# A product-key expert layer: tile 1 gathered by rows in place of tile 7, two tiles with scattered gates, and scatter indices loaded on GpSimd's queue

## The chip, the core and the metric

The kernel runs on one core of a Trainium2 chip. Its engines are TensorE (PE in the profile; PEld is its weight load), VectorE (DVE), ScalarE (ACT), GpSimd (POOL) and SyncE (SP, which here only issues DMAs). Each engine works through its own instructions in the order in which they were written to it, and waits for others by semaphores. The metric is the device time of one execution in microseconds.

## The reference

A one-layer encoder on 256 + 1024 tokens of width 1024: retention and latent attention (MLA) side by side, attention to 256 memory tokens, and a layer of single-neuron experts chosen by product keys (PEER). The expert layer is what the change touches. Per token:

```python
q = (xt @ wq).reshape(PEER_BLOCK, PEER_HEADS, PEER_QUERY_DIM)
s1 = jnp.einsum('thd,hkd->thk', q[..., :half], sub_keys[0])   # 8 heads x 128 keys
s2 = jnp.einsum('thd,hkd->thk', q[..., half:], sub_keys[1])
v1, i1 = lax.top_k(s1, 16); v2, i2 = lax.top_k(s2, 16)
cand = v1[..., :, None] + v2[..., None, :]
ts, sel = lax.top_k(cand.reshape(..., 256), 16)               # 16 experts a head, 128 a token
ids = take_along_axis(i1 * 128 + i2, sel); g = softmax(ts)
a = jnp.einsum('td,ted->te', xt, U[ids])
return jnp.einsum('te,ted->td', g * gelu(a), V[ids])          # U, V: 16384 x 1024
```

## The kernel before

The tokens are 10 tiles of 128: tiles 0 and 1 are the short group, 2 to 9 the long one. The program runs in stages:

- projection and retention of all tiles (`phase_a`), MLA of the short group, then "block 0" = tiles 0 and 1 (`phase_b`: output projection, memory attention, the expert layer's queries and scores);
- MLA of the long group (`phase_m`, g = 1), four pairs of heads, some 804 to 1248 us;
- block 1 = tiles 2 to 5 and block 2 = tiles 6 to 9 (`phase_b`);
- the gate stage (`gates`), some 1971 to 2212 us;
- the dense stage (`dense`), to the end.

After the scores of a tile are known, its **routing** (`lists`, `pairs`, `route`: top-16 twice, then the experts' numbers and gates) runs on VectorE. Then a tile takes one of three ways.

- **Gathered by rows** (GATHER, tiles 0, 7, 8, 9): for each of the token's 128 experts GpSimd issues one indirect DMA that brings a row of U to each of 128 partitions (tile `grow`, 4 buffers), and VectorE multiplies and sums it (`gj`); then the same with V (`gps`). That is 256 gathers a tile.
- **Over all experts** (DENSE, the other six): the dense stage computes U x for all 16384 experts on TensorE (`pa`), multiplies by a matrix of gates that is zero but for the chosen experts, and multiplies by V (`pv`, summed into `dacc`).
- The matrix of gates of a dense tile is made in one of two ways. With **scattered gates** (SCATTER, tiles 1, 2, 3) 128 indirect DMAs of GpSimd add each token's gates to a zeroed tensor GS in DRAM (`scatter`, line 1019); their indices and gates are first loaded to `sids` and `sg`, of which there is one buffer each. **On TensorE** (MADE, tiles 4, 5, 6) the gate stage makes, per token, two one-hot matrices (`o1`, `o2`) and one 128x128 matmul, and stores the result to G. Per group of four tokens `o1` is made on VectorE ("v") or ScalarE ("a") by the string O1_BY; `o2` is always VectorE's.

Routing, scatters and gathers are generators. `tick` is called from the main work with an estimate of TensorE's time and takes some steps of them at a share of it, routing first, scatters beside it; `gates` runs the routing of a tile to its end before it uses it, and `dense` runs what is left of the scatters before its first instruction. The order on each engine is then set by a scheduler of the tile framework that places instructions by its own simulated times; it is fixed when the program is built.

The gates of the last MADE tile are not sent through DRAM but kept in SBUF (`self.kept`); the first half of that tile's `pairs` is taken early. SyncE's queue issues nearly all loads and stores, in order: weights (`wraw`, `wl`), scores (`s`, `rs`), `ids`, `ii`, `sids`, `sg`, G, and in the dense stage U and V (`ur`, `vr`). In the dense stage `ur` and `vr` share four buffers, each of which GpSimd frees with its `ul` or `vl`.

Of the kernel before, what the change touches and what calls it, by code (L numbers as in the profile page):

```python
# [28 lines left out]
BLOCKS = [[0, 1], [2, 3, 4, 5], [6, 7, 8, 9]]  # L29
# [4 lines left out]
PH, PK, TK = 8, 128, 16  # L34
# [1 line left out]
EPS, GEPS = 1e-6, 1e-5  # L36
NDEC = RH * P + 5 * RH

GATHER = [0, 7, 8, 9]
DENSE = [t for t in range(NTILE) if t not in GATHER]  # L40
TD = len(DENSE) * P

SCATTER = [1, 2, 3]
MADE = [t for t in DENSE if t not in SCATTER]
TG = 64
HP = PK // 2
NG = 3
O1_BY = ("vaa", "va", "va")

RHO = ((0.75, 0.42), (0.5, 0.0), (0.9, 0.0))  # L50

# [56 lines left out]
class K:  # L108
# [550 lines left out]
    def phase_b(self, sd, blocks, before=None):  # L659

        nc, tc, I = self.nc, self.tc, self.I
        v = self.v
        width = max(len(ts) for ts in blocks) * P
        with ExitStack() as es:
# [74 lines left out]
            for ts in blocks:  # L739
# [95 lines left out]
                order = sorted(ts, key=lambda t: t in GATHER)  # L835
                with tc.tile_pool(name="brt", bufs=1, reuse_waits="tile") as kp:
                    for b in range(4):
                        keys = kp.tile([P, 4, P], F32, tag="keys", name=self.nm("keys"), bufs=2)
                        nc.scalar.dma_start(keys, I["keysT"][:, b * 4:b * 4 + 4, :])
                        ws = self.weights(room, I["peer_wq"], b * 512, 512, keep=kept("peer_wq", b))  # L840
                        qs = [kp.tile([P, 512], F32, tag="pq", name=self.nm("pq"), bufs=5) for j in range(4)]
                        for hf, tt, g, cols in halves:
                            if b == 0:
                                self.transposed(pp, xr[2 * hf:2 * hf + 2], part(a, cols), self.normw[:, 3, :])
                                for j, t in enumerate(tt):
                                    if t in GATHER:
                                        nc.sync.dma_start(sd["x3"][t], xr[2 * hf + j])
                                    else:
                                        sl = slice(hf * 256 + j * P, hf * 256 + (j + 1) * P)
                                        for i in range(2):  # L850
                                            nc.sync.dma_start(sd["x3T"][t][i], r32(a[i][:, :, sl]))

                            def ev(j, ps):
                                nc.scalar.copy(qs[j][:, cols], ps)  # L854
                            wstat(ws, a, cols, ev)
                        for j, t in enumerate(ts):
                            ps = ps_.tile([P, 4, P], F32, tag="s", name=self.nm("s"))
                            for h in range(4):
                                nc.tensor.matmul(ps[:, h, :], qs[h][:, j * P:(j + 1) * P], keys[:, h, :], start=True, stop=True)
                            s = kp.tile([P, 4, P], F32, tag="ks", name=self.nm("ks"), bufs=4)  # L860
                            nc.scalar.copy(s, ps)
                            nc.sync.dma_start(sd["s"][t][:, b * 4:b * 4 + 4, :], s)
                        if b < 3:
                            self.routing.append(self.lists(sd, order[0], b))
                            if b == 1 and order[0] == MADE[-1]:
                                self.routing.append(self.half(0))
                    self.routing.append(self.route(sd, order[0], 3))
                    for t in order[1:]:
# [93 lines left out]
    def route(self, sd, t, b0):  # L962


        nc = self.nc
        v = self.vf
        ap = self.rp
        for b in range(b0, 4):
            yield from self.lists(sd, t, b)
        yield from self.pairs(slice(PH // 2 if t == MADE[-1] else 0, PH))  # L970
        ts, ii = self.rt[3], self.rt[6]
        g = ap.tile([P, PH, TK], F32, tag="g", name=self.nm("g"))
        v.tensor_tensor(g, ts, ts[:, :, 0:1].broadcast_to([P, PH, TK]), ALU.subtract)
# [2 lines left out]
        v.tensor_reduce(sm, g, AX.X, ALU.add)  # L976
        v.reciprocal(sm, sm)
        v.tensor_tensor(g, g, sm.unsqueeze(2).broadcast_to([P, PH, TK]), ALU.mult)
        if t == MADE[-1]:

            self.kept = [ii[:, 0], ii[:, 1], g]
        else:
            nc.sync.dma_start(sd["g"][t], g.rearrange("p h k -> p (h k)"))
# [6 lines left out]
        else:  # L990
            if t in SCATTER:
# [6 lines left out]
                v.tensor_tensor(ids, ii[:, 0].rearrange("p h k -> p (h k)"), ii[:, 1].rearrange("p h k -> p (h k)"), ALU.add)  # L998
                nc.sync.dma_start(sd["ids"][t], ids)
                self.scattering.append(self.scatter(self.gp, sd, t))  # L1000
            elif t != MADE[-1]:
                nc.sync.dma_start(sd["ii"][t], ii.rearrange("p s h k -> p s (h k)"))
        self.routed.add(t)
        yield 0.8
# [2 lines left out]
    def scatter(self, gp, sd, t):  # L1007

        nc, tc = self.nc, self.tc
        ids = gp.tile([P, P], I32, tag="sids", name=self.nm("sids"), bufs=1)  # L1010
        nc.sync.dma_start(ids, sd["ids"][t])
        g = gp.tile([P, P], F32, tag="sg", name=self.nm("sg"), bufs=1)
        nc.sync.dma_start(g, sd["g"][t])
        before = self.zeroed[t]
        for h in range(PH):
            mine = []
# [88 lines left out]
    def gates(self, sd):  # L1105
# [3 lines left out]
        with ExitStack() as es:  # L1109
# [9 lines left out]
            for n, t in enumerate(MADE):  # L1119
                while t not in self.routed:  # L1120
                    self.step()
                if t == MADE[-1]:
                    r = [x.rearrange("p h k -> p (h k)") for x in self.kept]
                else:
                    rt = ap.tile([P, 3, P], F32, tag="r", name=self.nm("r"), bufs=2)
                    nc.sync.dma_start(rt[:, 0:2, :], sd["ii"][t])
                    nc.sync.dma_start(rt[:, 2, :], sd["g"][t])
                    r = [rt[:, j, :] for j in range(3)]
# [8 lines left out]
                for q in range(P // TG):  # L1137
                    st = ap.tile([P, HP, 2, TG], F32, tag="st", name=self.nm("st"), bufs=2)
                    self.late = self.anchor
                    for k in range(0, TG, 4):  # L1140
# [2 lines left out]
                        pt = pg.tile([P, 4, P], F32, tag="pt", name=self.nm("pt"))  # L1143
                        o1s = ap.tile([P, 4, P], F32, tag="o1", name=self.nm("o1"), bufs=6)
                        c0 = q * TG + k
                        by = O1_BY[n]
                        who = by[(c0 // 4) % len(by)]
                        if who == "v":
                            v.tensor_tensor(o1s, rT[:, 0, c0:c0 + 4].unsqueeze(2).broadcast_to([P, 4, P]),
# [245 lines left out]
```

## Time and profile before

| | |
|---|---|
| three runs | 4538.4, 4547.82, 4554.45 us, median 4547.82 us |
| profiled execution | 4537.65 us, of which span 4535.9 us |
| busy, share of the span | PE 87%, PEld 77%, DVE 68%, POOL 59%, ACT 33% |
| L1019, scatters | 384 instructions, 620.7 us of GpSimd |
| L1063, row gathers | 512 of U and 512 of V, 529.5 and 510.1 us of GpSimd |
| dense stage, matmuls `pa` and `pv` | 2048 and 1536 of each of three kinds, the same before and after the change |

A row of a view names the line, the engine, the operation and the tiles (out<-in, without buffer numbers). Busy times are of one engine; idle time stands with what ended it. An instruction is charged to the line that issued it; VectorE's go through two helpers, so that line 74 holds the main work and line 90 the routing and the gathers.

### The profile page before, as it was taken

Reading aid. Unit: us, or ns where it says so; the run is one execution under the profiler, and the core shown is the slowest. Engines: PE = TensorE matmul, PEld = TensorE weight load, DVE = VectorE, ACT = ScalarE, POOL = GpSimd, SP = SyncE. Lnnn points to the kernel's source line nnn. Section 1 sums busy time; section 2 is a strip of 40 time slices with the busy share of each in tenths; the row PEclk is TensorE's granted clock in tenths of the full one; section 3 lists DMA queues with packets and bytes.
Section 4 is the critical chain, followed back from the end, with each engine's and each line's share of the span. In section 5 each row is a group of like instructions: output and inputs, shape, how many; then the busy total and the mean of one; then the engine's idle time right before and its main releaser. Section 6 shows DMA issues by size and latency. Waiting matters only on the chain.

```text
span 4535.9 us, 64896 instructions
## 1 busy us (share of the span) xinstructions
PE 3937.6 (87%) x22425; PEld 3477.2 (77%) x22425; DVE 3073.4 (68%) x6808; ACT 1517.1 (33%) x3256; POOL 2677.9 (59%) x2283
## 2 busy tenths in 40 slices
PE   7999988856788989285599999999999999999998
PEld 7999867644577888274577888888888888888887
DVE  5565432844566498176399877777877777777778
ACT  5333544433434343065222222222222222222222
POOL 2230243178666557777436766776767777677775
PEclk9999998988899999698799999999999999999999
DMA  4422577124678867476637888989989989899887
GB/s 147 168 72 87 201 264 276 29 12 87 204 251 264 279 166 193 80 172 124 172 111 239 304 292 304 314 306 308 312 312 310 310 310 309 304 315 310 304 306 262
DMA packets 534843, 1030.49 MB, mean 227 GB/s; under 512 B 100848, under 2 KB 235504, under 8 KB 534512
## 3 DMA queue, kind: packets, MB, share of 16 engines
q0 software_dynamic: 204832, 545.55, 38.4%
q1 hardware_dynamic: 306928, 445.11, 30.0%
q10 hardware_dynamic: 22752, 35.68, 2.2%
q8 instruction: 176, 2.88, 0.3%
q14 instruction: 155, 1.27, 0.1%
HBM read 901.68 MB, written 124.45 MB: 226 GB/s over the span
## 4 chain that ended last, share of the span: by engine, by line
DMA 20%; POOL 14%; issue 11%; DVE 10%; PE 2%; ACT 1%; SPq 0%; POOLq 0%; DVEq 0%; ACTq 0%
DMA grow<-in_peer_v,gids 7%; DMA grow<-in_peer_u,gids 6%; POOL grow L1063 5%; POOL GS L1019 4%; DMA ur<-in_uT 3%; POOL vl L1245 3%; DVE gps L90 3%; POOL ul L1221 2%; DVE dacc L74 1%; DVE gj L90 1%; DVE oh L90 1%; DMA vr<-in_peer_v 1%; DVE wr L74 1%; DVE wl L74 1%; DMA GS<-sg,sids 1%
## 5 line engine op out<-in xcount | busy, mean ns | idle before, releaser
L1019 POOL DMA_INDIRECT GS<-sg,sids x384 | 620.7, 1616 | 314.6 <-DMA sids<-ids 142.7
L90 DVE SCALAR_TENSOR_TENSOR gps<-grow,ga,gps 128x1024 f32<-128x1024 f32 x512 | 657.4, 1284 | 218.4 <-DMA grow<-in_peer_v,gids 210.1
L1063 POOL DMA_INDIRECT grow<-in_peer_u,gids x512 | 529.5, 1034 | 354.1 <-DVE gj L90 222.2
L170 PE MATMUL pa<-dxT,uh 128*128 128x384 f32 x2048 | 690.0, 337 | 15.4 <-ACT uh L1220 12.8
L1063 POOL DMA_INDIRECT grow<-in_peer_v,gids x512 | 510.1, 996 | 321.8 <-DVE gps L90 206.1
L172 PE MATMUL pa<-dxT,ul 128*128 128x384 f32 x2048 | 682.1, 337 | 7.7 <-POOL ul L1221 7.4
L171 PE MATMUL pa<-dxT,uh 128*128 128x384 f32 x2048 | 688.0, 336 | 0.0
L170 PE MATMUL pv<-vh,wh 128*128 128x512 f32 x1536 | 612.0, 401 | 80.1 <-DVE dacc L74 73.4
L171 PE MATMUL pv<-vl,wh 128*128 128x512 f32 x1536 | 615.3, 401 | 20.6 <-POOL vl L1245 20.3
L172 PE MATMUL pv<-vh,wl 128*128 128x512 f32 x1536 | 607.6, 396 | 0.0
L90 DVE SCALAR_TENSOR_TENSOR gj<-grow,gps 128x1024 bf16<-128x1024 f32 x384 | 467.3, 1217 | 185.4 <-DMA grow<-in_peer_u,gids 170.7
L203 POOL TENSOR_TENSOR wl<-wraw,wh 128x512 fp32r<-128x512 f32 x180 | 239.5, 1349 | 342.8 <-ACT wh L199 241.4
L1221 POOL TENSOR_TENSOR ul<-ur,uh 128x512 fp32r<-128x512 f32 x256 | 338.3, 1329 | 148.6 <-ACT uh L1220 141.7
L170 PEld LDWEIGHTS pv<-vh,wh 128*128 128x128 f32 x1536 | 293.0, 191 | 165.2 <-DVE dacc L74 99.9
L170 PEld LDWEIGHTS pa<-dxT,uh 128*128 128x128 f32 x2048 | 386.2, 189 | 29.6 <-ACT uh L1220 17.0
L170 PE MATMUL pj<-act,wh 128*128 128x256 f32 x1088 | 311.6, 295 | 107.0 <-ACT pq L854 88.3
L172 PEld LDWEIGHTS pa<-dxT,ul 128*128 128x128 f32 x2048 | 385.1, 188 | 22.2 <-POOL ul L1221 19.0
L171 PEld LDWEIGHTS pa<-dxT,uh 128*128 128x128 f32 x2048 | 386.3, 189 | 4.2
L171 PEld LDWEIGHTS pv<-vl,wh 128*128 128x128 f32 x1536 | 293.1, 191 | 103.0 <-POOL vl L1245 49.7
L1245 POOL TENSOR_TENSOR vl<-vr,vh 128x512 fp32r<-128x512 f32 x256 | 328.3, 1301 | 68.6 <-ACT vh L1244 55.7
L90 DVE SCALAR_TENSOR_TENSOR gj<-grow,gx 128x1024 bf16<-128x1024 f32 x128 | 191.3, 1494 | 234.3 <-DMA grow<-in_peer_u,gids 233.0
L1220 ACT CAST uh<-ur 128x512 fp32r<-128x512 f32 x256 | 158.7, 621 | 550.0 <-DMA ur<-in_uT 517.9
(287 smaller groups left out, 8761.6 us busy)
## 6 DMA issues: line engine op xcount, KB each, us to landing
ur<-in_uT SPq DMA_DIRECT2D x256, 256.0 KB
vr<-in_peer_v SPq DMA_DIRECT2D x256, 256.0 KB
GS<-zero ACTq DMA_DIRECT2D x24, 1024.0 KB
wraw<-in_peer_wq SPq DMA_DIRECT2D x96, 256.0 KB
G<-st SPq DMA_DIRECT2D x48, 512.0 KB
gt<-GS SPq DMA_DIRECT2D x192, 128.0 KB
gt<-G SPq DMA_DIRECT2D x64, 384.0 KB
wraw<-in_w_out SPq DMA_DIRECT2D x48, 256.0 KB
```

The lines of the kernel that those rows point to most:

```text
L74: r = f(*a, **kw)
L90: r = f(*a, **kw)
L170: mm(ps, a[0], b[0], start=first, stop=False)
L171: mm(ps, a[0], b[1], start=False, stop=False)
L172: mm(ps, a[1], b[0], start=False, stop=last)
L203: (nc.vector if self.spare and k in self.spare else eng).tensor_tensor(wl[:, :n], raw[:, :n], r32(wh[:, :n]), ALU.subtract)
L1019: r = nc.gpsimd.indirect_dma_start(out=sd["GS"][t].rearrange("l a g h (t o) -> (l a g h t) o", o=1), in_=g[:, s:s + 1], in_offset=None, ou ...
L1063: nc.gpsimd.indirect_dma_start(out=u, out_offset=None, in_=src, in_offset=bass.IndirectOffsetOnAxis(ap=ids[:, s:s + 1], axis=0))
L1220: nc.scalar.copy(uh, ur)
L1221: nc.gpsimd.tensor_tensor(ul, ur, r32(uh), ALU.subtract)
L1245: nc.gpsimd.tensor_tensor(vl, vr, r32(vh), ALU.subtract)
```

## The change

Tile 1 changes places with tile 7: tile 1 is now gathered by rows, tile 7 goes over all experts with its gates made on TensorE. Two tiles (2, 3) have scattered gates in place of three, four (4 to 7) are made on TensorE in place of three. The tile whose `pairs` are halved (HALVED, still 6) and the one whose gates are kept in SBUF (KEPT, now 7) are no longer the same. `o1` is split evenly between VectorE and ScalarE for every tile. The loads of `sids` and `sg` move from SyncE's queue to GpSimd's.

```diff
-GATHER = [0, 7, 8, 9]
+GATHER = [0, 1, 8, 9]
...
-SCATTER = [1, 2, 3]
+SCATTER = [2, 3]
 MADE = [t for t in DENSE if t not in SCATTER]
+HALVED, KEPT = [t for t in MADE if t in BLOCKS[-1]][0], MADE[-1]
...
-O1_BY = ("vaa", "va", "va")
+O1_BY = "va"
...
-                            if b == 1 and order[0] == MADE[-1]:
+                            if b == 1 and order[0] == HALVED:
                                 self.routing.append(self.half(0))
...
-        yield from self.pairs(slice(PH // 2 if t == MADE[-1] else 0, PH))
+        yield from self.pairs(slice(PH // 2 if t == HALVED else 0, PH))
...
-        if t == MADE[-1]:
+        if t == KEPT:
             self.kept = [ii[:, 0], ii[:, 1], g]
...
         ids = gp.tile([P, P], I32, tag="sids", name=self.nm("sids"), bufs=1)
-        nc.sync.dma_start(ids, sd["ids"][t])
+        nc.gpsimd.dma_start(ids, sd["ids"][t])
         g = gp.tile([P, P], F32, tag="sg", name=self.nm("sg"), bufs=1)
-        nc.sync.dma_start(g, sd["g"][t])
+        nc.gpsimd.dma_start(g, sd["g"][t])
```

The order of the instructions moves at three places. The first is GpSimd's queue in the long group's MLA, behind its loads of the latents (`lat`). Before:

```order
L553 DMA lat_9615<-lat_69 128x768
L1019 DMA GS_183<-sg_10354,sids_10352 2097152x1 x64
L1063 DMA grow_11214<-in_peer_u,gids_11204 128x1024
L1063 DMA grow_11248<-in_peer_u,gids_11204 128x1024
L1063 DMA grow_11318<-in_peer_u,gids_11204 128x1024
L1063 DMA grow_11349<-in_peer_u,gids_11204 128x1024
L1019 DMA GS_183<-sg_10354,sids_10352 2097152x1 x13
L1063 DMA grow_11398<-in_peer_u,gids_11204 128x1024
```

Now (all line numbers are two higher):

```order
L555 DMA lat_9605<-lat_69 128x768
L1065 DMA grow_11178<-in_peer_u,gids_11168 128x1024
L1065 DMA grow_11211<-in_peer_u,gids_11168 128x1024
L1065 DMA grow_11280<-in_peer_u,gids_11168 128x1024
L1065 DMA grow_11310<-in_peer_u,gids_11168 128x1024
L1065 DMA grow_11358<-in_peer_u,gids_11168 128x1024
```

Tile 1's 128 scatters are gone from between tile 0's row gathers; 43 gathers stand in this stage before and after.

The second is SyncE's queue in block 2, while the expert layer's query weights are loaded. Before, the load of the third scatter's indices stands between these loads:

```order
L194 DMA wraw_19728<-in_peer_wq 128x512
L194 DMA wraw_19734<-in_peer_wq 128x512
L1011 DMA sids_22451<-ids_123 128x128
L194 DMA wraw_19740<-in_peer_wq 128x512
L1013 DMA sg_22453<-g_133 128x128
L983 DMA g_135<-g_19427 128x128
```

Now it stands on GpSimd's queue, between the last scatter of tile 2 and the first of tile 3:

```order
L1021 DMA GS_183<-sg_16710,sids_16708 2097152x1 x128
L1065 DMA grow_19518<-in_peer_u,gids_11168 128x1024
L1065 DMA grow_19906<-in_peer_u,gids_11168 128x1024
L1065 DMA grow_20098<-in_peer_u,gids_11168 128x1024
L1065 DMA grow_20129<-in_peer_u,gids_11168 128x1024
L1013 DMA sids_23088<-ids_123 128x128
L1015 DMA sg_23090<-g_133 128x128
L1065 DMA grow_20164<-in_peer_u,gids_11168 128x1024
L1065 DMA grow_20198<-in_peer_u,gids_11168 128x1024
L1021 DMA GS_184<-sg_23090,sids_23088 2097152x1 x2
L1065 DMA grow_20232<-in_peer_u,gids_11168 128x1024
L1021 DMA GS_184<-sg_23090,sids_23088 2097152x1 x11
```

In SyncE's queue six more loads of these weights now pass before the queue comes to a store (`ii` of tile 5) that needs VectorE's routing; before, `sids` was reached with 21 of this block's 32 loads issued, now `ii` with 27.

The third is VectorE's queue in the gate stage. The routing of tile 7, which before stood in the dense stage, now ends directly ahead of that tile's first one-hot matrices; the last rows of it now are

```order
L92 TENSOR_TENSOR oh_22436<-oh_22436 128x64x4
L92 TENSOR_TENSOR oh_22436<-oh_22436 128x64x2
L92 TENSOR_TENSOR ii_21896<-oh_22436 128x64
L76 TENSOR_SCALAR nT_22456<-rT_22454 128x128
L76 TENSOR_TENSOR o_4611_22464<-rT_22454,io 128x512
L76 TENSOR_SCALAR o_4612_22466<-io,rT_22454 128x128
```

Here `oh` and `ii` are the routing's last step and `nT` and `o` the gate stage's own. The number of row gathers inside the dense stage is the same, 125 of V of tile 0 and 256 for each of three tiles; the last of ScalarE's conversions that run ahead into the gate stage (`uh`, the third) stands behind 82 of 96 copies `st` before and behind 115 of 128 now.

## Rows read from the trace of the kernel before

**Rows 1.** The page's second part: the span in 40 slices of 113.4 us, busy tenths of TensorE and the clock that TensorE was granted.

```profile
PE   7999988856788989285599999999999999999998
PEclk9999998988899999698799999999999999999999
```

**Rows 2.** Busy time by stretch (stretch, its length, busy time of each engine with its count of instructions, granted clock, DMA share, GB/s): the four pairs of heads of the long group's attention, one stretch each.

```profile
804.00:886.00 82.00, 71.34 (x401) 52.03 (x400) 74.39 (x321) 43.61 (x81) 0.00 (x0) 0.94 0.08 25
886.00:966.00 80.00, 74.29 (x438) 53.59 (x438) 69.16 (x266) 42.98 (x82) 59.62 (x37) 0.96 0.28 26
966.00:1127.00 161.00, 78.06 (x432) 54.84 (x430) 53.38 (x102) 42.18 (x79) 131.52 (x87) 0.76 0.39 63
1127.00:1248.00 121.00, 96.33 (x515) 67.91 (x514) 66.85 (x126) 49.18 (x96) 76.20 (x58) 0.87 0.67 193
```

**Rows 3.** From 886 to 1183 us, while the first scatter runs: what VectorE waited for (total us, times, longest), and GpSimd's two groups of instructions (count, busy us, mean ns, idle time before them).

```profile
DVE gj L90 <- DMA grow<-in_peer_u,gids: 111.2, 16, 50.2
L1019 POOL DMA_INDIRECT GS<-sg,sids x128 | 209.5, 1637 | 152.8 <-DMA sids<-ids 107.1 <-issue 43.1 <-DMA GS<-sg,sids 1.6
L1063 POOL DMA_INDIRECT grow<-in_peer_u,gids x27 | 28.8, 1065 | 8.2 <-issue 7.3 <-DMA GS<-sg,sids 0.6 <-DVE ob L74 0.3
```

**Rows 4.** In order of time (start us, length us, then what; in brackets the idle time before it and what ended it): GpSimd's first row gather, and the VectorE instruction that waited for that gather.

```profile
1017.79 1.00 POOL L1063 DMA_INDIRECT grow<-in_peer_u,gids  x1 [0.30 <-issue]
...
1022.22 1.23 DVE L90 SCALAR_TENSOR_TENSOR gj<-grow,gx 128x1024 bf16<-128x1024 f32 x1 [50.23 <-DMA grow<-in_peer_u,gids]
```

**Rows 5.** Waits from 1500 to 1910 us (who, for whom, total us, times, longest us), the engines' and SyncE's queue.

```profile
DVE gj L90 <- DMA grow<-in_peer_u,gids: 106.0, 4, 93.7
ACT wh L199 <- DMA wraw<-in_peer_wq: 104.8, 12, 87.6
...
SPq L1011 <- DMA GS<-sg,sids: 95.2, 4, 89.8
```

**Rows 6.** In order of time: the first and the last instruction of the second scatter and the first of the third on GpSimd; SyncE's load of the third scatter's indices; and VectorE's first instruction of the gate stage.

```profile
1632.52 1.63 POOL L1019 DMA_INDIRECT GS<-sg,sids  x1 [35.63 <-DMA sids<-ids]
...
1898.88 1.54 POOL L1019 DMA_INDIRECT GS<-sg,sids  x1 [0.30 <-issue]
1913.93 1.89 POOL L1019 DMA_INDIRECT GS<-sg,sids  x1 [0.30 <-issue]
...
1901.95 0.33 SPq L1011 DMA_DIRECT2D sids<-ids  x1
...
1978.87 0.23 DVE L74 TENSOR_SCALAR nT<-rT 128x128 f32<-128x128 f32 x1 [18.14 <-ACT rT L1133]
```

**Rows 7.** Busy time by stretch, columns as in rows 2: the gate stage before, in and after its stop.

```profile
1975.00:2112.00 137.00, 106.62 (x697) 92.79 (x697) 133.06 (x497) 126.86 (x334) 100.60 (x62) 0.93 0.81 185
2112.00:2197.00 85.00, 0.65 (x3) 0.65 (x4) 0.81 (x3) 1.81 (x5) 64.99 (x43) 0.51 0.26 14
2197.00:2215.00 18.00, 17.30 (x112) 16.65 (x112) 14.01 (x62) 12.94 (x33) 0.16 (x1) 0.87 0.96 276
```

**Rows 8.** The gate stage's groups (count, busy us, mean ns, idle time before): one-hot halves and copies on ScalarE, both one-hot halves on VectorE.

```profile
L74 DVE TENSOR_SCALAR o<-io,rT 128x128 f32<-128x128 f32 x384 | 108.6, 363 | 85.1 <-PE pt L1164 84.4
L74 DVE TENSOR_TENSOR o<-rT,io 128x512 f32<-128x512 f32 x43 | 29.2, 679 | 0.0
L1157 ACT ACTIVATE o<-io,nT 128x128 f32<-128x128 f32 x212 | 69.4, 416 | 0.3 <-DVE nT L74 0.3
L1158 ACT ACTIVATE o<-o 128x512 f32<-128x512 f32 x53 | 33.8, 646 | 0.0
L1166 ACT COPY st<-pt 128x512 f32<-128x512 f32 x96 | 55.1, 597 | 4.0 <-DMA G<-st 1.9 <-PE pt L1164 1.4
```

**Rows 9.** Around the gate stage's stop: a wait of SyncE's queue (2090 to 2200 us), and the scatter's instructions with VectorE busy (2000 to 2090 us, first row) and idle (2113 to 2192 us, second row).

```profile
SPq L1217 <- POOL ul L1221: 93.8, 2, 92.2
...
L1019 POOL DMA_INDIRECT GS<-sg,sids x43 | 72.0, 1674 | 20.6 <-issue 12.5 <-DMA GS<-sg,sids 8.2
...
L1019 POOL DMA_INDIRECT GS<-sg,sids x40 | 61.7, 1542 | 17.8 <-issue 15.4 <-DMA GS<-sg,sids 2.5
```

**Rows 10.** In order of time: the last scatter instruction on GpSimd, and VectorE's last instruction of the gate stage and its first of the dense stage.

```profile
2189.35 1.54 POOL L1019 DMA_INDIRECT GS<-sg,sids  x1 [0.30 <-issue]
...
2211.58 0.28 DVE L90 FIND_INDEX8 ti<-tv,rs 128x8 uint32<-128x128 f32 x1
2231.35 2.23 DVE L74 TENSOR_TENSOR wr<-wr,gt 128x384 f32<-128x384 f32 x2 [19.48 <-DMA gt<-GS]
```

**Rows 11.** Busy time of VectorE in the instructions of line 90 alone, over the whole span, and the page's three groups of that line that belong to the gathers.

```profile
0.00:4540.00 4540.00, 1792.21 (x3969) 0.94 0.71 227
...
L90 DVE SCALAR_TENSOR_TENSOR gps<-grow,ga,gps 128x1024 f32<-128x1024 f32 x512 | 657.4, 1284 | 218.4 <-DMA grow<-in_peer_v,gids 210.1
L90 DVE SCALAR_TENSOR_TENSOR gj<-grow,gps 128x1024 bf16<-128x1024 f32 x384 | 467.3, 1217 | 185.4 <-DMA grow<-in_peer_u,gids 170.7
L90 DVE SCALAR_TENSOR_TENSOR gj<-grow,gx 128x1024 bf16<-128x1024 f32 x128 | 191.3, 1494 | 234.3 <-DMA grow<-in_peer_u,gids 233.0
```

**Rows 12.** Busy time by stretch, columns as in rows 2: two stretches of the dense stage.

```profile
2235.00:3000.00 765.00, 716.33 (x3484) 635.40 (x3485) 632.41 (x1314) 195.96 (x355) 471.35 (x417) 0.97 0.78 263
3000.00:4000.00 1000.00, 953.38 (x4685) 839.76 (x4684) 773.70 (x934) 255.81 (x467) 704.73 (x647) 0.99 0.90 308
```

**Rows 13.** One line's instructions on one tensor (count, shortest, median and longest in ns, first and last start in us): plain loads that GpSimd issues.

```profile
L553 POOL DMA_DIRECT2D lat<-lat x8: 537/538/573, 771.0 to 783.8; - x8
```

More of the change, by code (lines that the diff above doesn't have):

```diff
@@ L1000, in route @@
                 self.scattering.append(self.scatter(self.gp, sd, t))
-            elif t != MADE[-1]:
+            elif t != KEPT:
                 nc.sync.dma_start(sd["ii"][t], ii.rearrange("p s h k -> p s (h k)"))
@@ L1121, in gates @@
                     self.step()
-                if t == MADE[-1]:
+                if t == KEPT:
                     r = [x.rearrange("p h k -> p (h k)") for x in self.kept]
@@ L1145, in gates @@
                         c0 = q * TG + k
-                        by = O1_BY[n]
+                        by = O1_BY
                         who = by[(c0 // 4) % len(by)]
```

## The prediction

> **What bounds the kernel now.** I read the page's slices first. TensorE is busy eight or nine tenths almost throughout, with two kinds of holes: two slices near 1000 us at five and six tenths and slices at about 1870 and 2160 us at two and five, and the granted clock falls there too [rows 1]. The dense stage, from slice 21 on, is full. So the question is what the change does to these holes and what it adds.
>
> The first hole is in the long group's attention. Its four pairs of heads are the same work, but take 82, 80, 161 and 121 us [rows 2]. What differs is in the waits of VectorE: it waits 111.2 us, 16 times, for rows of U [rows 3]. These rows are gathered on GpSimd, and in its queue tile 1's scatter stands ahead of and between the gathers: 128 instructions of 1637 ns against 27 gathers of 1065 ns [rows 3]. The first gather starts at 1017.79 us, and VectorE, which reached its use about 50 us earlier, goes on at 1022.22 [rows 4]. VectorE works in order, so the softmax behind that product waits too, and TensorE with it.
>
> The second hole is in block 2. SyncE waits 89.8 us to load the third tile's indices, because `sids` has one buffer and the second scatter is still reading it; behind it in the queue are the query weights, and ScalarE waits 87.6 us for those [rows 5]. But VectorE is held in the same time as well, 93.7 us, by one row gather [rows 5] that stands in GpSimd's queue behind the same 128 scatters. The scatter runs from 1632.52 to 1898.88, the indices are loaded at 1901.95, the gate stage begins at 1978.87 [rows 6].
>
> The third hole, 85 us, is in the gate stage [rows 7]: SyncE waits 92.2 us for GpSimd to free a buffer of `ur` [rows 9], and GpSimd does so only behind the third scatter, at 2189.35 [rows 10]. ScalarE's `uh` for that load stands ahead of the last copies of the gates, so the gates stop.
>
> **Term 1, tile 1's scatter: -100 us.** All 128 scatters go from the attention stage; nothing takes their place there, since tile 1's rows are gathered in the dense stage, where tile 7's were. Two readings price it: VectorE's waits, 111.2 us [rows 3], and the pace, 161 + 121 against 82 + 80, that is 120 us [rows 2]. Pace is the upper end, since it also counts the product instructions themselves. What is late next is the gathers' own latency: 4.4 us from the first one's start to its use [rows 4], hidden by four buffers when 41 gathers are spread over some 170 us. I take 100, a little under the waits, because VectorE will wait for some of the 27. The low end is 50: only the first long wait goes, and the others covered something else on TensorE or ScalarE.
>
> **Term 2, the indices on GpSimd's queue: -10 us at the start of the gate stage, and +2.** This removes SyncE's wait but not VectorE's: the row gather still stands behind the second scatter. In the new order SyncE gets six more of this block's weight loads out and then stops at a store that needs VectorE. So the hole becomes shorter by TensorE's work on six of 32 loads, and what it can give the gate stage is bounded by the 18.14 us that VectorE waited there for TensorE's late end of the block [rows 6]. I take 10 of 0 to 18, as one row gather now stands behind 13 scatters of the third tile, where it stood behind 7. GpSimd's four new loads cost 538 ns each [rows 13], 2 us in all; behind each wait scatters and gathers, and the landing they wait for is the one that they waited for before. The whole hole counted as gain, 84 us, would be a mistake: the end of the next stage hangs on the scatters, which start no earlier relative to block 1.
>
> **Term 3, a fourth tile of gates and tile 7's routing: +20 us.** VectorE was busy 133.06 + 14.01 us in the gate stage [rows 7]. Added are one tile of `o2`, 108.6 / 3 = 36 us; 64 in place of 43 `o1`, 21 x 679 ns = 14 us [rows 8]; and a tile's routing, line 90 less its gathers over ten tiles, (1792.2 - 657.4 - 467.3 - 191.3) / 10 = 48 us [rows 11]. Together 245 us. ScalarE has less: for a tile 16 of its `o1` at (69.4 + 33.8) / 53 = 1.95 us and copies of 55.1 / 3 = 18 us, 50 us, four times 200 [rows 8]; so VectorE sets the stage. Before, the stage took 1978.87 to 2211.58 [rows 6, 10], 233 us, with 85 of them the stop. The new work fills the stop. Counted from the second scatter's last instruction (1898.88), the gates begin at +70, `uh` is reached after 115 of 128 copies at +70 + 220 = +290, and the third scatter ends at +290 before, some +300 now; so a stop of about 10 us is left. The stage takes 245 + 10 = 255, 22 more than before; I count 20. Low end 0 (the model of VectorE is too full), high end 97: none of the new work fits into the stop.
>
> A rule of the Trainium skill speaks against this step. Scatters with VectorE busy take 1674 ns and with it idle 1542 [rows 9]; 128 of them all under the gates make at most 17 us, of which the third scatter bore more than half already, and the +300 holds the rest. The page "SBUF — State Buffer", section "SBUF: two separate sides", says that a DMA issued by GpSimd needs descriptors written by it, and that some two-port VectorE instructions lock it out meanwhile, so that such a DMA belongs on another queue. By that the scatter would stretch further under four tiles of `o2`, and the stop grow; by the rows it costs 0.13 us an instruction.
>
> **Term 4, the dense stage: -3 us.** TensorE's work and the number of gathers are unchanged, and a tile's routing less stands on VectorE. In the first stretch, with three routings, 3484 matmuls take 765 us, at the later pace (4685 in 1000 us) they would take 744 [rows 12]: 21 us, 7 for each routing at most, 0 at least. I take 3.
>
> **The sum.** -100 - 10 + 2 + 20 - 3 = -91 on the profiled execution, 4537.65 us, of which 4535.9 are span: 4447 us. That execution is 10 us below the median of the three runs and just below their fastest; I move up by 3 and say 4450.
>
> **Rivals.**
>
> 1. The gate stage's stop stays whole. It would if the third scatter ended some 75 us later against the gates than I count, or if another `ur` stood in front of earlier copies. For it: the same queues meet there as before. Against: 115 of 128 copies now stand ahead of `uh`. The price is the other 75 us of the 85: 4525. Chance 0.09.
> 2. Only the first wait in the attention stage goes (50 of the 100 us): 4500. For it: TensorE has only 78 us of work in the 161 of the third pair, so something else could be late next. Against: the first two pairs ran in 82 and 80 us with VectorE busy 74 and 69 of them [rows 2]. Chance 0.12.
> 3. The hole in block 2 closes, because VectorE reaches the held gather later than TensorE needs it. Then the gates end before the third scatter, and that bounds: the stage ends at +300 and a few copies in place of +325, 25 us earlier: 4425. Chance 0.09.
> 4. Slower. The attention stage's pace is set by the landing of the gathered rows and not by their place behind the scatters, so that term 1 gives 10 at most, while the fourth tile's gates and the routing (98 us) lie open behind the stop: 4537.65 - 10 + 97 = 4625. It decides where term 1 is smaller than term 3. For it: a wait that is put down to a DMA may be the transfer itself. Against: the gather of 1017.79 had landed 4.4 us later [rows 4]. Chance 0.04.
>
> That the change does not do what it says is excluded for the attention stage by the order; for the hole in block 2 it is what term 2 says.
>
> **How the numbers follow.** The forecast has 0.66: its own spread is -120 to -80 for term 1 and 0 to +30 for term 3, so 4417 to 4480. The range, 4405 to 4500, takes in rivals 2 and 3 and the sum with 50 or 120 for term 1; rivals 1 and 4 lie outside. Runs of this kernel differ by about 0.3%, 14 us, and less than that counts as the same: 4534 to 4561. All cases but rival 4 lie below 4534, and of rival 1 (4525) a third may reach it: faster 0.92, same 0.04, slower 0.04.
>
> **What will show it.** The four pairs of heads should take some 80 us each, with VectorE's waits for rows of U under 20 us there. The second scatter should start some 100 us earlier, at about 1532. VectorE should still wait about 90 us for one row gather in block 2, and TensorE still stop, for 40 to 70 us, with SyncE now at the store of `ii`. The gate stage should have VectorE busy for about 245 us with a stop of at most 20 us. The dense stage should start 75 to 100 us earlier and last as long as before, within 10 us. The prediction is wrong if the third pair still takes over 110 us, if the gate stage still stops for over 50, or if the dense stage changes by more than 20.

## The result and the profile after

| | before | after |
|---|---|---|
| median of the runs (us) | 4551.14 (4538.4 to 4557.76) | 4433.91 (4422.06 to 4437.58) |
| ratio to before, 95% interval | | 0.9741 (0.9712 to 0.977) |
| profiled execution (us), its span | 4537.65, 4535.9 | 4435.69, 4433.9 |
| PE busy | 3937.6 (87%) | 3971.3 (90%) |
| GpSimd busy | 2677.9 (59%) | 2475.2 (56%) |

The change made the kernel faster, by 117 us in the medians and by 102 us between the two profiled executions. The kernel before has a fourth run here, beside the three given above. The line numbers of after are two higher than those of before. The page's slices of after, TensorE and the clock granted to it (they answer to [rows 1]):

```profile
PE   7999888899889986476899999999999999999998
PEclk9999999899899998688999999999999999999999
```

The hole at slices 8 and 9 (counted from 0) is gone, and the clock no longer falls there. Of the other two, the one at 18 and 19, the gate stage's stop, has become a stage with TensorE at seven and six tenths (slices 17 and 18); the one in block 2 stays, in slices 15 and 16, about 1740 to 1860 us. Four places of the trace show where the 102 us went.

**The attention of the long group.** Its four pairs of heads by stretch, each from one pair's first instruction to the next one's (stretch, length, busy time of PE, PEld, DVE, ACT and POOL with counts, granted clock, DMA share, GB/s), as in [rows 2]:

```profile
806.00:889.00 83.00, 70.99 (x405) 51.21 (x404) 75.06 (x328) 43.91 (x81) 0.05 (x1) 0.94 0.09 26
889.00:967.00 78.00, 72.87 (x431) 52.73 (x430) 70.89 (x264) 42.45 (x81) 7.21 (x8) 0.96 0.20 64
967.00:1040.00 73.00, 70.93 (x434) 51.01 (x433) 53.91 (x105) 43.46 (x81) 20.25 (x18) 1.00 0.45 139
1040.00:1138.00 98.00, 87.10 (x517) 62.66 (x515) 60.18 (x116) 48.63 (x95) 32.63 (x29) 0.95 0.67 224
```

Together 332 us, where it was 444. The waits from 889 to 1138 us (who, for whom, total us, times, longest), the stretch that answers to [rows 3], and GpSimd's first gather (start, length; in brackets the idle time before it):

```profile
POOL grow L1065 <- DMA gids<-ids: 102.3, 1, 102.3
POOL grow L1065 <- DVE st L76: 73.7, 9, 52.7
...
DVE ob L76 <- ACT ob L595: 20.5, 8, 3.6
...
888.95 1.01 POOL L1065 DMA_INDIRECT grow<-in_peer_u,gids  x1 [102.32 <-DMA gids<-ids]
```

VectorE's wait for rows of U, 111.2 us before, no longer appears, and its longest total is the 20.5 us shown; now GpSimd waits for VectorE. The gather that started at 1017.79 [rows 4] starts at 888.95.

**Block 2.** Waits from 1390 to 1830 us, of the engines and of SyncE's queue, which answer to [rows 5]:

```profile
DVE gj L92 <- DMA grow<-in_peer_u,gids: 110.3, 10, 96.5
ACT wh L201 <- DMA wraw<-in_peer_wq: 104.6, 13, 84.6
PE pj L172 <- ACT pq L856: 84.0, 4, 82.4
...
SPq L1004 <- DVE ii L92: 93.8, 1, 93.8
```

TensorE still stops for 82.4 us. The instructions around this stop in order of time, from the timelines of GpSimd, VectorE and SyncE's queue, as in [rows 6]: the second scatter's first and last instruction, VectorE's held product, GpSimd's loads of the indices and gates, the third scatter's first, SyncE's held store, and VectorE's first instruction of the gate stage:

```profile
1515.52 1.65 POOL L1021 DMA_INDIRECT GS<-sg,sids  x1 [3.65 <-DMA sids<-ids]
...
1791.20 1.55 POOL L1021 DMA_INDIRECT GS<-sg,sids  x1 [0.30 <-issue]
...
1797.47 1.23 DVE L92 SCALAR_TENSOR_TENSOR gj<-grow,gx 128x1024 bf16<-128x1024 f32 x1 [96.52 <-DMA grow<-in_peer_u,gids]
...
1797.83 0.62 POOL L1013 DMA_DIRECT2D sids<-ids  x1
1798.41 0.63 POOL L1015 DMA_DIRECT2D sg<-g  x1
...
1803.95 1.62 POOL L1021 DMA_INDIRECT GS<-sg,sids  x1 [0.56 <-DMA sg<-g]
...
1812.59 0.32 SPq L1004 DMA_DIRECT2D ii<-ii  x1
...
1862.30 0.23 DVE L76 TENSOR_SCALAR nT<-rT 128x128 f32<-128x128 f32 x1 [7.48 <-ACT rT L1135]
```

SyncE's queue no longer stops at `sids` but, for 93.8 us, at the store of `ii`, which needs VectorE's routing, and VectorE stands at a row gather behind the scatter, as before.

**The gate stage.** The whole stage as one stretch, its groups (count, busy us, mean ns, idle time before; the last is the scatters), and GpSimd's last scatter and VectorE's first product of the dense stage; they answer to [rows 7], [rows 8] and [rows 10]:

```profile
1862.00:2107.00 245.00, 175.90 (x1069) 152.59 (x1068) 238.76 (x950) 181.75 (x460) 173.73 (x106) 0.86 0.74 167
...
L76 DVE TENSOR_SCALAR o<-io,rT 128x128 f32<-128x128 f32 x512 | 149.1, 368 | 0.2
L76 DVE TENSOR_TENSOR o<-rT,io 128x512 f32<-128x512 f32 x64 | 43.3, 678 | 0.0
L1021 POOL DMA_INDIRECT GS<-sg,sids x103 | 170.1, 1652 | 43.3 <-issue 28.3 <-DMA GS<-sg,sids 14.7 <-PE pt L1166 0.3
...
2072.92 1.55 POOL L1021 DMA_INDIRECT GS<-sg,sids  x1 [0.30 <-issue]
...
2123.87 1.03 DVE L76 TENSOR_TENSOR wr<-wr,gt 128x384 f32<-128x384 f32 x2 [18.95 <-DMA gt<-G]
```

The stop of 85 us [rows 7] is gone: VectorE is busy 238.76 of 245 us, and its one-hots wait 0.2 us where they waited 85.1 [rows 8]. From the stage's first instruction to the dense stage's first product it is 261.6 us, where it was 252.5 [rows 6, 10].

**The dense stage.** Two stretches of it, as in [rows 12], and TensorE's last matmul:

```profile
2128.00:2893.00 765.00, 722.84 (x3538) 641.33 (x3539) 616.04 (x1098) 195.71 (x357) 492.31 (x441) 0.98 0.82 278
2893.00:3893.00 1000.00, 944.06 (x4618) 830.38 (x4617) 767.43 (x938) 253.02 (x458) 697.76 (x641) 0.99 0.89 304
...
4425.23 0.39 PE L174 MATMUL pv<-vh,wl 128*128 128x512 f32 x1
```

Against before, the stages begin or end as follows (start of the matmuls behind the attention 1252.97 and 1138.63; before's last matmul ended at 4527.84; the others from the rows above and [rows 6, 10]):

| | before | after | difference |
|---|---|---|---|
| block 1 begins on TensorE | 1252.97 | 1138.63 | -114.3 |
| second scatter's first instruction | 1632.52 | 1515.52 | -117.0 |
| second scatter's last instruction | 1898.88 | 1791.20 | -107.7 |
| gate stage, VectorE's first | 1978.87 | 1862.30 | -116.6 |
| dense stage, VectorE's first | 2231.35 | 2123.87 | -107.5 |
| TensorE's last matmul ends | 4527.84 | 4425.62 | -102.2 |

So the whole gain is made before 1253 us; the gate stage gives 9 us back and the dense stage 5.

### The profile page after: what moved, and what is told of

Read it like the earlier page. It is cut to its first block, busy times and chain, and to the rows that moved or that the text cites. A ratio compares the mean times of both kernels' runs of the same rounds, so it can differ in the third digit from the quotient of the medians.

```text
span 4433.9 us, 65461 instructions
## 1 busy us (share of the span) xinstructions
PE 3971.3 (90%) x22684; PEld 3508.8 (79%) x22684; DVE 3111.2 (70%) x6954; ACT 1558.1 (35%) x3344; POOL 2475.2 (56%) x2159
## 5 line engine op out<-in xcount | busy, mean ns | idle before, releaser
L1021 POOL DMA_INDIRECT GS<-sg,sids x256 | 420.1, 1641 | 123.6 <-issue 97.7
L174 PEld LDWEIGHTS pv<-vh,wl 128*128 128x128 f32 x1536 | 294.2, 192 | 57.3
L1237 ACT CAST wh<-wr 128x384 fp32r<-128x384 f32 x256 | 130.7, 513 | 580.9 <-DVE wr L76 575.4
```

Source lines behind the costliest of these rows:

```text
L174: mm(ps, a[1], b[0], start=False, stop=last)
L1021: r = nc.gpsimd.indirect_dma_start(out=sd["GS"][t].rearrange("l a g h (t o) -> (l a g h t) o", o=1), in_=g[:, s:s + 1], in_offset=None, ou ...
L1237: nc.scalar.copy(wh, wr)
```

## The experiments

Ratios are to the kernel before, run on the same chip beside each group of four.

### Where the gain comes from: the queue of the index loads, or tile 1's scatter

The first kernel undoes one part of the change:

```diff
-        nc.gpsimd.dma_start(ids, sd["ids"][t])
+        nc.sync.dma_start(ids, sd["ids"][t])
...
-        nc.gpsimd.dma_start(g, sd["g"][t])
+        nc.sync.dma_start(g, sd["g"][t])
```

> The changed kernel with the scatter indices and gates loaded on SyncE's queue again, as before the change. Theory: VectorE's row gather behind the second scatter holds block 2 whichever queue the indices are on, so this costs 0 to 10 us: 4434 to 4445 us, ratio to the kernel before 0.974 to 0.977, TensorE's stop in block 2 again about 84 us and starting some 20 us earlier against the end of the second scatter. Rival: SyncE's wait was what held block 2, and moving the loads is worth most of the 84 us: 4500 to 4515 us, ratio 0.989 to 0.992.

It took 4434.45 us, ratio 0.9744 (0.9718 to 0.977): no different from the changed kernel. Its waits from 1390 to 1860 us, and TensorE's first matmul behind the stop in block 2: before, in the changed kernel, and here (in brackets the stop):

```profile
DVE gj L92 <- DMA grow<-in_peer_u,gids: 126.4, 13, 95.3
SPq L1013 <- DMA GS<-sg,sids: 94.8, 4, 89.3
...
1908.80 0.58 PE L170 MATMUL pj<-act,wh 128*128 128x256 f32 x1 [83.90 <-ACT pq L854]
...
1822.37 0.58 PE L172 MATMUL pj<-act,wh 128*128 128x256 f32 x1 [82.43 <-ACT pq L856]
...
1794.29 0.58 PE L174 MATMUL pj<-act,wl 128*128 128x256 f32 x1 [83.86 <-DMA wl<-wl_peer_wq]
```

TensorE's stop is 83.9 us, where it is 82.4 in the changed kernel, and the gates begin at 1861.5. What differs is where the stop lies against the second scatter's last instruction (1898.88 before, 1791.20 in the changed kernel, 1783.80 here). Before and here it runs from 74 and 73 us ahead of that instruction to 10 us behind it; in the changed kernel, from 51 us ahead to 31 us behind. So the six weight loads do make the stop begin 22 us later, as expected, but it also ends 21 us later. With the loads on SyncE the queue goes on as soon as the scatter has ended; in the changed kernel it goes on at 1812.59, when VectorE has done the routing that stands behind the gather of 1797.47. The move of the loads shifts the stop and does not shorten it, and in the time it is worth nothing that these runs show.

The second takes the kernel before and leaves out tile 1's 128 scatters alone:

```diff
-                self.scattering.append(self.scatter(self.gp, sd, t))
+                if t == 1:
+                    self.scattered[t] = self.zeroed[t]
+                else:
+                    self.scattering.append(self.scatter(self.gp, sd, t))
```

> The kernel before with the 128 scatter instructions of tile 1 left out, so that tile 1's gates stay zero; nothing else is changed. Theory: the attention stage becomes 105 to 117 us shorter and all that follows comes earlier by that and lasts as long as before: 4434 to 4446 us, ratio 0.974 to 0.977. Rival: the attention stage's gain is partly eaten later, because the chain of the two other scatters does not move along: 4480 to 4500 us, ratio 0.985 to 0.989.

4432.51 us, 0.9748 (0.9719 to 0.9777). Leaving out the one scatter gives as much as the whole change. But the work behind it is different: here the gate stage has three tiles and still stops. Its waits from 1860 to 2110 us:

```profile
PE pt L1167 <- ACT st L1169: 86.3, 3, 85.7
ACT uh L1223 <- DMA ur<-in_uT: 85.7, 1, 85.7
```

Its dense stage begins at 2117.30, only 6.6 us before that of the changed kernel. So the fourth tile of gates and a tile's routing, 98 us of VectorE by the prediction's count, fill a stop of 85 and cost 7 on top (10 if each stage is counted from its own first instruction).

### What bounds the stages between: the held gather, the third scatter, or VectorE

The third kernel takes no row gathers into GpSimd's order while a scatter is under way (in two places):

```diff
-        while self.owed > 0.0 and (self.routing or self.gathering):
+        while self.owed > 0.0 and (self.routing or self.gathering and not self.scattering):
```

> The changed kernel with no row gathers taken up while a scatter is pending, so that nine gathers of U move behind the third scatter. Theory: VectorE is not held in block 2, TensorE's stop of 82 us there goes and the gate stage starts some 80 us earlier, but the third scatter still ends where it did (10 us earlier at most), the gate stage stops for it again, and the dense stage starts 40 us behind it, as in the kernel before: 15 to 20 us gained, 4410 to 4420 us, ratio 0.969 to 0.971. Rival A: the scatters are no bound, and the 82 us come through: 4350 us, ratio 0.956. Rival B: something else holds block 2: 4434 us, ratio 0.974.

4427.84 us, 0.9741 (0.9711 to 0.9771). The stop in block 2 is gone and the gates begin 87 us earlier, at 1775.3. They then stop for the third scatter, whose last instruction starts at 2070.64: ScalarE's `uh` waits for a load of `ur`, whose buffer GpSimd frees behind the scatter. The gate stage by stretch, before and in this stop, and that wait:

```profile
1775.00:2004.00 229.00, 160.59 (x961) 135.67 (x960) 221.93 (x887) 167.20 (x424) 171.53 (x104) 0.87 0.69 150
2004.00:2079.00 75.00, 0.00 (x0) 0.00 (x0) 2.03 (x7) 2.49 (x7) 57.51 (x38) 0.53 0.25 19
...
ACT uh L1222 <- DMA ur<-in_uT: 75.0, 1, 75.0
```

The dense stage begins at 2114.27, 9.6 us earlier than in the changed kernel. Of 82 us of stop removed in block 2, 75 come back in the gate stage. The bound is the theory's. Of the 15 to 20 us that it gave, the start of the dense stage shows about half and the time none: the ratio is that of the changed kernel, 0.9741.

The fifth kernel (the fourth comes below) is this one with the index loads on SyncE again, the edit of the first experiment.

> The kernel without the held gather (e3) with the scatter indices and gates on SyncE's queue. Theory: two waits cover each other in block 2, VectorE's gather and SyncE's index load; with the first gone the second alone holds the weights, so that TensorE's stop of some 80 us in block 2 is back, and the gate stage starts at about 1855 us and not at 1775. The time grows little, since the third scatter bounds the stage's end: 4428 to 4440 us, ratio 0.973 to 0.976. Rival: with VectorE free there is no stop in block 2 on either queue, and the time is that of e3, 4428 us, with gates from 1775 us.

4426.4 us, 0.9729 (0.968 to 0.9778). TensorE's longest wait from 1390 to 1860 us (of its weight loads), SyncE's from 1500 to 1900 us, and the gate stage as one stretch:

```profile
PEld pj L174 <- DMA wl<-wl_peer_wq: 78.7, 2, 77.6
...
SPq L1013 <- DMA GS<-sg,sids: 86.0, 4, 80.6
...
1858.00:2105.00 247.00, 177.06 (x1063) 151.25 (x1063) 238.91 (x950) 181.21 (x458) 163.27 (x99) 0.87 0.71 162
```

The stop in block 2 is back at 77.6 us, with no gather held. So two waits covered one another there: VectorE's for the gather and SyncE's for `sids`. Each keeps the stop alone, VectorE's in the changed kernel and SyncE's in this run, and only with both gone does it close (the third). The total does not tell the two kernels apart, but not for the reason expected. In this one the gates begin at 1857.8, VectorE is busy 238.91 of 247 us, and the third scatter's last instruction starts at 2062.19: as in the changed kernel VectorE's gates come last, and the dense stage begins at 2123.7. In the third kernel the gates begin 83 us earlier, the third scatter comes last, and the dense stage begins 9.5 us earlier.

The fourth kernel is the changed one with less work in the last tile's gates: of every 64 tokens only the first four get one-hots and matmuls, and the gates of the others are copies of theirs.

```diff
-                        pt = pg.tile([P, 4, P], F32, tag="pt", name=self.nm("pt"))
-                        o1s = ap.tile([P, 4, P], F32, tag="o1", name=self.nm("o1"), bufs=6)
+                        if not (t == KEPT and k):
+                            pt = pg.tile([P, 4, P], F32, tag="pt", name=self.nm("pt"))
+                            o1s = ap.tile([P, 4, P], F32, tag="o1", name=self.nm("o1"), bufs=6)
...
+                        if t == KEPT and k:
+                            nc.scalar.copy(st[:, :, :, k:k + 4], st[:, :, :, 0:4])
+                            continue
```

> The changed kernel with most of tile 7's gates left out: of every 64 tokens only the first four get one-hot matrices and matmuls, and their result is copied for the others; routing, copies and stores stay. Theory: VectorE has 44 us less in the gate stage, but the third scatter then bounds, so that the dense stage starts 40 us behind its end: 10 us gained, 4420 to 4428 us, ratio 0.971 to 0.973. Rival A: VectorE alone sets the stage's end: 44 us gained, 4390 us, ratio 0.965. Rival B: the gates' work was wholly covered: 4434 us.

4418.05 us, 0.9703 (0.9674 to 0.9732). VectorE's first product of the dense stage, the last scatter, and two stretches of SyncE's queue:

```profile
2104.45 2.11 DVE L76 TENSOR_TENSOR wr<-wr,gt 128x384 f32<-128x384 f32 x2 [40.29 <-DMA gt<-GS]
...
2073.73 1.55 POOL L1021 DMA_INDIRECT GS<-sg,sids  x1 [0.30 <-issue]
...
2067.84 27.00 SPq L1120 DMA_DIRECT2D G<-st  x16
...
2098.32 0.95 SPq L1216 DMA_DIRECT2D gt<-GS  x2
```

VectorE now waits 40 us for the scattered gates, and the dense stage begins 19 us earlier than in the changed kernel; the time falls by 16, which the two intervals do not separate. So in the changed kernel VectorE's gates come last. The size lies between what the theory and the rival expected, nearer the theory, but the theory's bound is not what shows. The third scatter's last instruction has ended at 2075.28, and the first loads of the scattered gates are issued at 2098.32, behind 16 stores of G that keep SyncE's queue busy for 27 us. The edit left these stores in and let them come all at once. How far the third scatter's chain lies behind VectorE's gates in the changed kernel is not shown by this run; that it bounds when the gates begin 87 us earlier is shown by the third.

### A version without the second bound

In the third kernel VectorE stands still for 75 us until the third scatter has ended. Making that tile's gates on TensorE too puts work in the place of the stop and takes away what it waits for. The sixth kernel is the third with one scattered tile and five made on TensorE:

```diff
-SCATTER = [2, 3]
+SCATTER = [2]
```

> e3 with tile 3's gates made on TensorE too: one tile with scattered gates, five on TensorE. Theory: with the third scatter gone VectorE sets the gate stage's end; from 1775 us 245 + 36 + 11 = 292 us, then some 19 us to the dense stage's first product, 2086 us against 2114 in e3: 28 us gained, 4400 us, ratio 0.967. Rival: the fifth tile's gates cost as much as they free, because SyncE's stores of G bound the stage: 4428 us or above, ratio 0.974 or more.

4388.26 us, 0.9647 (0.9612 to 0.9681), about 46 us under the changed kernel and 40 under the third, where 28 were expected; the dense stage begins at 2070.83, 43 us earlier than in the third. The gate stage as one stretch, its VectorE group from 1760 to 2070 us, and the page's slices:

```profile
1772.00:2052.00 280.00, 210.43 (x1312) 184.65 (x1313) 277.91 (x1092) 224.83 (x571) 19.80 (x13) 0.90 0.63 174
...
L76 DVE TENSOR_SCALAR o<-io,rT 128x128 f32<-128x128 f32 x640 | 178.9, 340 | 0.3
...
PE   7999988899898999777999999999999999999998
PEclk9999999899999999988999999999999999999999
```

No slice falls under seven tenths any more, and in the gate stage VectorE is busy 277.91 of 280 us: it sets the stage. I had expected 292 us. Of the 12 us between, 6 are in the count I began with, 245 us of VectorE where the changed kernel had 239. Some 7 are in the one-hots, which with GpSimd nearly idle took 280 ns of busy time each (178.9 us for 640) against 291 in the changed kernel, beside scatters (149.1 us for 512). The means of the rows, 340 and 368 ns, are spans that overlap, as 512 times 368 ns is more than the 149.1 us.

The last two kernels move VectorE's part of the one-hot half `o1` to GpSimd, all of it in the seventh and half of it in the eighth:

```diff
-O1_BY = "va"
+O1_BY = "ap"
```

> e6 with VectorE's half of the one-hot matrices o1 made on GpSimd, four instructions of 128x128 for a group of four tokens. Theory: VectorE has 80 x 0.68 = 54 us less and ScalarE's 250 us set the stage's end; dense stage from about 2045 us: 40 us gained on e6, 4360 us, ratio 0.958. Rival: GpSimd takes over 1 us for each of the 320 instructions and sets the end at 2095 us or later: no gain on e6, 4400 to 4420 us, ratio 0.967 to 0.972.

```diff
-O1_BY = "va"
+O1_BY = "vapa"
```

> e6 with a quarter of the o1 groups on VectorE, a half on ScalarE and a quarter on GpSimd. Theory: VectorE has 27 us less: dense stage from about 2060 us, 25 us gained on e6, 4375 us, ratio 0.962. Rival: GpSimd's and VectorE's one-hot instructions slow each other, and nothing is gained on e6: 4400 us, ratio 0.967.

The seventh took 4385.41 us, 0.9631 (0.9599 to 0.9664), the eighth 4398.86 us, 0.9666 (0.9633 to 0.9699); neither can be told from the sixth, and the gains of 40 and 25 us that the theories gave did not come. All three beat both kernels of the change. In the seventh the dense stage begins 8 us earlier (2062.7), in the eighth no earlier (2072.0). Groups of the seventh from 1760 to 2070 us:

```profile
L1155 POOL TENSOR_SCALAR o<-io,rT 128x128 f32<-128x128 f32 x320 | 201.3, 805 | 38.5 <-PE pt L1166 21.5 <-ACT rT L1135 16.7
L1166 PE MATMUL pt<-o,o 128*128 128x128 f32 x1280 | 196.8, 305 | 51.6 <-POOL o L1155 18.5 <-DVE o L76 15.5 <-ACT o L1160 13.4
L76 DVE TENSOR_SCALAR o<-io,rT 128x128 f32<-128x128 f32 x640 | 192.2, 366 | 17.5 <-PE pt L1166 16.8
```

VectorE gave up 54 us of work, but its remaining one-hots kept it busy for 192.2 us in place of 178.9, and it now waits 16.8 us for TensorE. TensorE in turn waits for three engines, for GpSimd longest. That little comes of it because no single engine sets the stage any more fits these rows; it was not tried by itself.

## Why the prediction was right

**The time.** 4450 was forecast, 4433.91 measured, inside the range; and the sign was right. The sum of the terms for the profiled execution was -91, and it came to -102. That it is only 11 us off is in part luck: terms 1 and 3 came out 14 and 11 us better than forecast, terms 2 and 4 came out 6 and 8 us worse. Three signs lay outside what I had written: the fourth pair took 98 us and not some 80, TensorE's stop in block 2 82 us and not 40 to 70, and the dense stage began 107.5 us earlier and not 75 to 100. And the low end of the forecast's own spread was added wrongly: -120 for term 1 and 0 for term 3 give 4410, not 4417.

**Term 1, tile 1's scatter, -100: right in kind, too small by 14.** The next stage starts 114.3 us earlier, and leaving out the scatter alone gives the whole gain (second experiment). I chose a value under VectorE's waits (111.2) because some of 27 gathers would still be waited for; none is, to speak of. Either reading by itself was nearer than that value, the waits by 3 us and the pace, 120, by 6. (The prediction spreads 41 gathers where the order has 43; nothing hangs on it.) The pace holds something that the waits do not: with the stop gone the granted clock of the third and fourth pair rose from 0.76 and 0.87 to 1.00 and 0.95, of the full 2.4 GHz, and nearly the same matmuls took 70.93 + 87.10 us of TensorE, where they took 78.06 + 96.33 [rows 2], 16 us less. That this is what the 14 us consist of was not tried by itself.

**Term 2, the index loads, -10 and +2: the step failed, though its small sum did no harm.** I had the stop become shorter "by TensorE's work on six of 32 loads", 40 to 70 us. It is 82.4, and with the loads on SyncE 83.9. The six loads do pass and the stop begins 22 us later for it, but it ends 21 us later as well (first experiment): SyncE now waits for VectorE's routing, and that stands behind the gather that hangs on the scatter, as I had written one sentence earlier. I counted the later start and did not ask for the end. The gates do begin 9 us earlier relative to the scatter's last instruction (71.1 us behind it, before 80.0), but the scatter itself took 9 us longer, so nothing was gained. The two new loads of GpSimd behind the second scatter cost 0.62 and 0.63 us each there; the 2 us for all four were of the right size.

**Term 3, the fourth tile of gates, +20: right in kind, too high by 11.** VectorE set the stage as the sum said, busy 238.76 us where I had 245, with o2 at 149.1 us for four tiles and o1 at 43.3. The 10 us of remaining stop did not come: the third scatter's last instruction came at 2072.92, 282 us behind the second's last, earlier than the +300 of the prediction, and ScalarE reached the third `uh` only at 2086.13, so that nothing waited. The page "SBUF — State Buffer" of the Trainium skill, section "SBUF: two separate sides", spoke against this step. The scatters under the four tiles took 1652 ns in the mean, 0.11 us more than the 1542 ns with VectorE idle [rows 9], and no stop grew out of it; that the scatters are locked out for the length of VectorE's instructions, as the page has it for those with two ports, these rows do not show.

**Term 4, the dense stage, -3: open.** It took 2301.8 us where it took 2296.5. In its first 765 us VectorE had 16 us less to do, a third of the routing that moved, and 54 more matmuls were done than before; in the next 1000 us 67 fewer were done [rows 12]. At that later pace this is 12 us won and 14 lost again; why the second stretch is slower was not tried. And runs of one kernel differ by 15 us, so whether the 5 us are real is not settled.

**The rivals.** The gate stage's stop did not stay (rival 1). All of the attention stage's waits went, not only the first (rival 2). Block 2's hole did not close (rival 3); where I made it close, in the third experiment, the third scatter bounded the gates as rival 3 had it, at 10 us of gain in the dense stage's start and not 25. The attention stage was not set by the landing of the rows (rival 4): with the scatter gone, VectorE no longer waited for them.

## What to carry to other kernels

The price of work on an in-order queue is not its busy time but the wait of what stands behind it: 209 us of scatter on an engine with time to spare cost 114 us, since another engine's rows queued behind it. Where two waits cover the same hole, removing one shows nothing; remove both, and then look for the third chain that ends just behind. A large stop can take new work nearly free: 98 us of VectorE went into one of 85 for 7 to 10 us. But the next bounds stood close behind: gates that began 87 us earlier brought the dense stage 10 us nearer, and 42 us less of VectorE's work in the gates (196 us for 239) brought it 19 nearer. The next gain that the time shows, 46 us, came in the kernel where the third scatter was taken away and VectorE's gates began earlier as well; the scatter's removal alone was not tried.

## What the runs showed of the hardware beyond what I expected

VectorE's 128x128 one-hot comparison differs in cost with what GpSimd does beside it. In busy time one costs 280 ns with GpSimd nearly idle (sixth run), 291 beside scatters (149.1 us for 512, the changed kernel) and 300 beside GpSimd's own one-hots (192.2 us for 640, seventh run). GpSimd has 629 ns of busy time for the same instruction (201.3 us for 320). There the two were busy for 201 and 192 us within the same 310, so for at least 83 us together: VectorE is slowed by about 7% and not shut out.

Beside GpSimd's subtraction `ul` it is shut out. Two stretches of the changed kernel's gate stage, the second and the third row being single instructions of VectorE:

```profile
2079.53 2.81 POOL L1223 TENSOR_TENSOR ul<-ur,uh 128x512 fp32r<-128x512 f32 x2 [5.06 <-ACT uh L1222]
...
2081.12 1.30 DVE L76 TENSOR_SCALAR o<-io,rT 128x128 f32<-128x128 f32 x1
...
2082.35 0.34 DVE L76 TENSOR_SCALAR o<-io,rT 128x128 f32<-128x128 f32 x1
```

The comparison that starts inside GpSimd's second subtraction takes 1.30 us and ends 0.08 us behind it; the next one takes 0.34 us. Eighteen comparisons start inside an `ul` in the traces of the changed kernel and of the first, fifth, sixth, seventh and eighth kernels, three in each, and all do so: they take 1.20 to 1.31 us and end 0.08 us behind GpSimd.

The second scatter is the same work in both kernels, but its 128 instructions took 204.1 us before and 208.5 after, with 36.0 and 62.3 us of idle time ahead of them that no wait explains (GpSimd's group in the stretch of that scatter, before and after):

```profile
L1019 POOL DMA_INDIRECT GS<-sg,sids x128 | 204.1, 1595 | 99.4 <-issue 36.0 <-DMA sids<-ids 35.6 <-DMA GS<-sg,sids 27.8
...
L1021 POOL DMA_INDIRECT GS<-sg,sids x128 | 208.5, 1629 | 72.4 <-issue 62.3 <-DMA GS<-sg,sids 6.4 <-DMA sids<-ids 3.7
```

The waits for the scatter's own earlier transfers shrank meanwhile, from 27.8 to 6.4 us. Busy time and idle time behind the first instruction together grew by 9 us; why was not tried.
